# Attention scores of two key heads in 64-row halves of the TensorE array

## The chip, the cores and the metric

The kernel runs on one core of a Trainium2 chip. A core has TensorE (PE: matmuls, with its weight loads shown apart as PEld), VectorE (DVE), ScalarE (ACT), GpSimd (POOL) and SyncE (SP, which here issues the DMAs). TensorE writes into PSUM, eight banks of 128 rows by 512 f32 values; the others work from SBUF, and VectorE and ScalarE also read PSUM. The metric is the device time of one execution in microseconds.

## The reference

One layer of a decoder that runs windowed attention beside a state-space branch, then a gated feed-forward part with a short convolution, for a prompt of 2048 tokens and eight samples of four tokens. The attention of the prompt, which is what the change touches, is this (cut):

```python
qb = q.reshape(b, nb, BLOCK, N_KV_HEADS, GQA_GROUP, HEAD_DIM)   # 16 blocks of 128, 2 key heads, 4 query heads each, 64
kband = jnp.concatenate([kb[:, :-1], kb[:, 1:]], axis=2)        # the block before and this one: 256 keys
s = jnp.einsum('bnqhgd,bnkhd->bnhgqk', qb, kband) * scale
s = s - slopes * dist                                           # ALiBi
s = jnp.where(valid, s, MASK_VALUE)
p = _sink_softmax(s, sinks)
o = jnp.einsum('bnhgqk,bnkhd->bnqhgd', p.astype(v.dtype), vband)
```

`_sink_softmax` subtracts the maximum over the keys and the head's sink, takes the exponential, and divides by the sum with the sink's exponential added.

## The kernel before

The kernel works through stages. First it projects the inputs of the state-space branch for all tokens. Then, between about 150 and 530 us, it interleaves four kinds of work: the projections of queries, keys and values in tiles of 256 tokens, the state-space branch in 16 pairs of groups, the attention in 16 blocks of 128 queries, and, towards the end, the activations, the gate (`glu`) and the sample attention. Behind it come the output projection and the feed-forward part, which take the rest of the time and which the change does not touch.

**The order.** The interleaving is written out by hand. Each kind of work is a Python generator that is cut into steps by `yield`, and the string `ORDER` names one step after another: `q` the next step of the projections, `s5` the next step of pair 5 of the state-space branch, `a4` the next step of attention block 4, `g` a step of the gate, `x` of the sample attention, `e` of the activations, `Y` the loads for those. TensorE's instructions run in just this order (`manual_schedule` for that engine). The instructions of the other engines are ordered by the compiler's planner, by their place in the program and by what is ready; on each engine they then run in order. The numbers that the generators yield are not read when the order is written out.

**An attention block** (`attention_block`, L523) has five steps:

1. scores of key head 0 for its four query heads, their eviction, and the softmax of head 0;
2. the same for key head 1;
3. transposes of head 0's probabilities (`tp_b`, L556), eight of them in two banks, and copies to SBUF (`pT`);
4. the same for head 1;
5. the product with the values (`o`, L567), its copy and its DMA out.

**Scores.** A query tile holds, for each of four positions j, 128 rows: the 64 values of query head j of key head 0, and below them the 64 values of query head j of key head 1. To pick one key head out of it, the keys are padded: `kpad[i][:, kv, :]` has 128 rows of which the 64 of the other key head are zero. So a matmul takes all 128 rows with 256 keys as the moving side. Queries and keys are each split into a high and a low part (two fp32r tiles, index i), and `mm3` (L87) issues three matmuls into the same columns of a PSUM bank: high x high, high x low, low x high. A bank `sc` holds two query heads of 256 keys; there are two such banks. VectorE evicts each half bank with one operation (L545) that adds the bias, takes the maximum with the sink, and writes scores `s` and maximum `m`.

**Softmax** (`softmax`, L506) of one key head: VectorE negates the maximum (`ngm`), ScalarE takes four exponentials with their sums (L513), VectorE forms the sink's share and the reciprocal (`es`, `den`), and GpSimd multiplies the four heads (L520). Only then can the transposes of step 3 or 4 start. The `s` tiles lie in four buffers, so block b uses those of block b-2 again.

**Keys.** `kpads` (L840 on) are two pairs of key tiles of 384 keys each, used in turn by tiles of 256 tokens. GpSimd fills the rows of the other head with zeros once, and in the first pair also the 128 keys ahead of the prompt. The keys of each tile are then written by ScalarE and VectorE into the 64 rows of their head (L912 on), and GpSimd copies the last 128 keys of the tile before.

**The sample attention** (`sample_attention`) computes its scores in tiles of 64 rows by 32 columns of the array (L604), with the keyword `tile_position`, in f32.

## Time and profile before

| | |
|---|---|
| time, median of 3 runs | 2193.05 us (2192.98 to 2195.53) |
| the profiled execution's own time | 2194.39 us |
| its span, first to last instruction | 2192.2 us |
| mean granted TensorE clock | 0.973 |
| busy: PE / DVE / ACT / POOL | 2054.4 / 1307.6 / 1055.8 / 1208.9 us |

In the profile a row of the timeline gives start, length, engine, line, operation, output<-inputs, the form (rows*columns of the array for TensorE, then the output), and in brackets the idle time before it with what ended it. A TensorE instruction's length includes the way through the array, so that consecutive ones overlap; the distance of their starts is what one costs, and the chain of waits shows just that distance. The page's busy time of TensorE is a union of such lengths.

### The profile page before, as it was taken

The numbers are of one execution on the slowest core, as the hardware profiler recorded it, in microseconds if no ns is written. First come the engines' busy times: TensorE is split into PE (matmuls) and PEld (weight loads), VectorE is DVE, ScalarE is ACT, GpSimd is POOL, SyncE is SP. The second block draws the span as 40 slices with busy tenths as digits, with TensorE's granted clock in tenths as the row PEclk, the third lists the DMA queues.
The fourth block names the chain that finished last, engine by engine and source line by source line (L and its number), as shares of the span: only waits on it lengthen the run. The fifth ranks groups of instructions, "written<-read, shape, count | busy, mean of one in ns | idle before, by whom it ended". The sixth has DMA issues, their size and how long they took to land.

```text
span 2192.2 us, 41498 instructions
## 1 busy us (share of the span) xinstructions
PE 2054.4 (94%) x14685; PEld 1923.5 (88%) x14685; DVE 1307.6 (60%) x3298; ACT 1055.8 (48%) x2467; POOL 1208.9 (55%) x1196
## 2 busy tenths in 40 slices
PE   8969999968999979999999998999999999999997
PEld 8967878857998979999999786779999999888997
DVE  8859998458565576766766265227766766601231
ACT  6525465665454456666666332225655655612011
POOL 4857776334356776666665553446666666823121
PEclk9989999989999989999999999999999999999999
DMA  8865434686488733333334795834333333584643
GB/s 232 240 169 158 116 106 138 125 230 189 146 248 258 262 109 109 113 95 109 114 95 128 263 284 170 303 117 157 110 93 108 111 93 108 177 205 125 199 132 95
DMA packets 294352, 347.59 MB, mean 159 GB/s; under 512 B 42344, under 2 KB 250864, under 8 KB 294128
## 3 DMA queue, kind: packets, MB, share of 16 engines
q1 hardware_dynamic: 294144, 344.94, 52.3%
q8 instruction: 116, 1.90, 0.4%
q14 instruction: 92, 0.75, 0.1%
HBM read 232.70 MB, written 107.80 MB: 155 GB/s over the span
## 4 chain that ended last, share of the span: by engine, by line
PE 75%; DVE 8%; DMA 6%; issue 4%; ACT 3%; POOL 3%; SPq 2%; DVEq 0%; ACTq 0%; POOLq 0%
PE ux L1362 21%; PE u L1362 16%; PE dn L90 6%; PE dn L89 6%; PE dn L91 6%; PE wo L90 2%; PE wo L91 2%; PE wo L89 2%; PE qkv L89 2%; PE qkv L91 1%; PE qkv L90 1%; DVE xo L1444 1%; SPq L802 1%; PE u L91 1%; DMA mt<-mscr 1%
## 5 line engine op out<-in xcount | busy, mean ns | idle before, releaser
L84 POOL TENSOR_TENSOR wdl<-wdr,wdh 128x1024 fp32r<-128x1024 f32 x65 | 159.3, 2455 | 287.3 <-ACT wdh L83 272.0
L89 PE MATMUL dn<-ah,wdh 128*128 128x512 f32 (+3 forms) x552 | 205.6, 372 | 8.9 <-DMA ah<-actscr 3.6
L91 PE MATMUL dn<-ah,wdl 128*128 128x512 f32 (+3 forms) x552 | 205.1, 371 | 3.3 <-POOL wdl L84 3.3
L90 PE MATMUL dn<-al,wdh 128*128 128x512 f32 (+3 forms) x552 | 204.9, 371 | 0.5 <-DMA al<-actscr 0.5
L1327 ACT ACTIVATE cc<-u,cw 128x260 f32<-128x260 f32 (+1 forms) x252 | 141.5, 563 | 93.8 <-DVE u L1405 64.1
L1519 DVE TENSOR_TENSOR xo<-xo,dn 128x512 f32<-128x512 f32 (+3 forms) x40 | 21.9, 584 | 265.4 <-PE dn L91 265.1
L83 ACT CAST wdh<-wdr 128x1024 fp32r<-128x1024 f32 x65 | 68.0, 1050 | 230.4 <-PE dn L90 188.4
L84 POOL TENSOR_TENSOR wls<-s,whs 128x1024 fp32r<-128x1024 f32 x42 | 100.9, 2402 | 133.2 <-ACT whs L83 133.2
L1328 DVE SCALAR_TENSOR_TENSOR cc<-u,cw,cc 128x260 f32<-128x260 f32 (+1 forms) x252 | 121.0, 481 | 64.2 <-ACT cc L1327 62.7
L89 PE MATMUL wo<-mh,wo 128*128 128x260 f32 x512 | 149.0, 291 | 2.5 <-ACT mh L83 2.5
L90 PE MATMUL wo<-ml,wo 128*128 128x260 f32 x512 | 146.7, 287 | 1.5 <-POOL ml L84 1.3
L91 PE MATMUL wo<-mh,wo 128*128 128x260 f32 x512 | 146.4, 286 | 0.0
L1405 DVE TENSOR_TENSOR u<-u,cb 128x262 f32<-128x262 f32 x84 | 36.5, 435 | 158.5 <-PE u L1362 158.5
L89 PEld LDWEIGHTS dn<-ah,wdh 128*128 128x128 f32 x552 | 105.1, 190 | 28.7 <-issue 4.0
L91 PEld LDWEIGHTS dn<-ah,wdl 128*128 128x128 f32 x552 | 105.1, 190 | 20.8 <-POOL wdl L84 4.2
L89 PE MATMUL qkv<-hh_p,wqh 128*128 128x256 f32 (+1 forms) x384 | 113.5, 296 | 10.6 <-DVE vs L905 7.4
L84 POOL TENSOR_TENSOR wlt<-s,wht 128x512 fp32r<-128x512 f32 x42 | 54.1, 1288 | 122.6 <-ACT wht L83 64.0
L90 PEld LDWEIGHTS dn<-al,wdh 128*128 128x128 f32 x552 | 105.1, 190 | 17.6 <-DMA al<-actscr 1.0
L1329 DVE SCALAR_TENSOR_TENSOR cc<-u,cw,cc 128x260 f32<-128x260 f32 (+1 forms) x252 | 119.6, 475 | 0.8
L84 POOL TENSOR_TENSOR wlg<-wur,whg 128x1024 fp32r<-128x1024 f32 x42 | 101.1, 2407 | 27.8 <-ACT whg L83 27.8
L520 POOL TENSOR_SCALAR s_b<-s_b,den_b 128x256 f32<-128x256 f32 x128 | 75.4, 605 | 63.2 <-DVE den_b L518 38.4
L90 PE MATMUL qkv<-hl_p,wqh 128*128 128x256 f32 (+1 forms) x384 | 109.9, 286 | 0.0
(574 smaller groups left out, 8370.9 us busy)
## 6 DMA issues: line engine op xcount, KB each, us to landing
actscr<-cc SPq DMA_DIRECT2D x168, 260.0 KB, 4.9
wur<-in_w_up SPq DMA_DIRECT2D x84, 512.0 KB, 4.1
wdr<-in_w_down SPq DMA_DIRECT2D x77, 512.0 KB, 4.9
x<-in_xT SPq DMA_DIRECT2D x56, 256.0 KB, 4.2
hs<-h2scr SPq DMA_DIRECT2D x44, 262.0 KB, 4.6
ah<-actscr SPq DMA_DIRECT2D x42, 256.0 KB, 3.9
al<-actscr SPq DMA_DIRECT2D x42, 256.0 KB, 4.2
mt<-mscr SPq DMA_DIRECT2D x16, 520.0 KB, 5.5
```

Of the source, the lines that this page charges most:

```text
L83: i = nc.scalar.copy(hi, src) if hi_eng is nc.scalar else hi_eng.tensor_copy(hi, src)
L84: return i.ins, lo_eng.tensor_tensor(lo, src, hi.bitcast(F32), ALU.subtract).ins
L89: nc.tensor.matmul(ps, w[0], x[0], start=first, stop=False)
L90: nc.tensor.matmul(ps, w[0], x[1], start=False, stop=False)
L91: nc.tensor.matmul(ps, w[1], x[0], start=False, stop=last)
L520: nc.gpsimd.tensor_scalar(s[:, h], s[:, h], den[:, h : h + 1], 1.0, ALU.mult, ALU.mult)
L802: nc.sync.dma_start(uscr[8 * m + g].rearrange("(s h) c -> h s c", h=16), uperm[m][16 * g : 16 * g + 16])
L1327: nc.scalar.activation(cp, pp[:, 2:], AF.Identity, bias=w[3], scale=w[2])
L1328: nc.vector.scalar_tensor_tensor(cp, pp[:, 1 : npr + 1], w[1], cp, ALU.mult, ALU.add)
L1329: nc.vector.scalar_tensor_tensor(cp, pp[:, 0:npr], w[0], cp, ALU.mult, ALU.add)
L1362: nc.tensor.matmul(pt[:, :W], x[p][:, k], y[q][:, k], start=start and k + i == 0, stop=k == 3 and i == 2, skip_group_check=True)
L1405: v.tensor_tensor(c21[s], c21[s], cb[s][:, 0], ALU.add)
```

## The change

Both key heads' scores are now computed in one step. A matmul takes 64 rows: those of its key head, from the query tile and from the key tile, at the matching half of the array's rows (`tile_position=(64 * kv, 0)`). For two query heads of each key head the matmuls of key head 0 and key head 1 alternate, each into a bank of its own. The first step of a block covers query positions 0 and 1 of both key heads, the second positions 2 and 3; the softmax of both key heads is called in the second step. The number of matmuls, their 256 moving columns, the evictions, the softmax and the later steps stay as they were, and so does `ORDER`. The maxima `m` get eight buffers instead of three. The zeros in the other head's rows are not written any more; those ahead of the prompt are.

```diff
-    ss, pts = [], {}
+    ss, ms, pts = [], [], {}
     for kv in range(2):
         nm = f"b{b}_{kv}"
         s = pool.tile([P, 4, 256], F32, tag="s", name=f"s_{nm}", bufs=4)
-        m = pool.tile([P, 4], F32, tag="m", name=f"m_{nm}", bufs=3)
+        ms.append(pool.tile([P, 4], F32, tag="m", name=f"m_{nm}", bufs=8))
         if b == 0:
             v.memset(s[:, :, 0:P], MASK)
-        for hh in range(2):
-            pt = ps.tile([P, 512], F32, tag="sc", name=f"sc_{nm}_{hh}")
-            for h2 in range(2):
-                j = 2 * hh + h2
-                q = [qhl[i][:, j, qb : qb + P] for i in range(2)]
-                k = [kpad[i][:, kv, kb : kb + 256] for i in range(2)]
-                mm3(nc, pt[:, 256 * h2 : 256 * h2 + 256], q, k, True, True)
+        ss.append(s)
+    for hh in range(2):
+        sc = [ps.tile([P, 512], F32, tag="sc", name=f"sc_b{b}_{kv}_{hh}") for kv in range(2)]
+        for h2 in range(2):
+            for i, (x, y) in enumerate(((0, 0), (0, 1), (1, 0))):
+                for kv in range(2):
+                    r = slice(64 * kv, 64 * kv + 64)
+                    nc.tensor.matmul(sc[kv][:, 256 * h2 : 256 * h2 + 256], qhl[x][r, 2 * hh + h2, qb : qb + P],
+                                     kpad[y][r, kv, kb : kb + 256], start=i == 0, stop=i == 2, tile_position=(64 * kv, 0))
+        for kv in range(2):
+            s, m, pt = ss[kv], ms[kv], sc[kv]
             for h2 in range(2):
                 j = 2 * hh + h2
                 lo = P if b == 0 else 0
...
-        softmax(c, pool, s, m, 4, c.sink[:, 4 * kv : 4 * kv + 4], nm)
-        ss.append(s)
+            if hh:
+                softmax(c, pool, s, m, 4, c.sink[:, 4 * kv : 4 * kv + 4], f"b{b}_{kv}")
         yield 1.4
...
-            for t in kp:
+            for t in kp if i == 0 else ():
                 f = t.bitcast(F32)
-                nc.gpsimd.memset(f[64:128, 0, :], 0.0)
-                nc.gpsimd.memset(f[0:64, 1, :], 0.0)
-                if i == 0:
-                    nc.gpsimd.memset(f[0:64, 0, 0:P], 0.0)
-                    nc.gpsimd.memset(f[64:128, 1, 0:P], 0.0)
+                nc.gpsimd.memset(f[0:64, 0, 0:P], 0.0)
+                nc.gpsimd.memset(f[64:128, 1, 0:P], 0.0)
```

## The prediction

> **What bounds the kernel now.** I read the page's head first, then a table of stretches of the span, then the chain of waits between 160 and 530 us (start, length, what), then the instructions that touch the score tile `sc_b`.

> ```profile
> span 2192.2 us, 41498 instructions
> ```

> The stretches (their length, then busy us of PE, PEld, DVE, ACT and POOL, granted clock, DMA share, GB/s):

> ```profile
> 177.00:227.00 50.00, 45.65 (x318) 35.55 (x314) 49.62 (x163) 28.99 (x95) 36.95 (x71) 1.00 0.43 122
> 227.00:408.00 181.00, 178.92 (x1300) 150.07 (x1301) 154.82 (x499) 97.05 (x307) 117.89 (x222) 1.00 0.41 117
> 408.00:530.00 122.00, 98.25 (x719) 82.92 (x717) 70.79 (x203) 83.78 (x203) 47.31 (x72) 0.92 0.80 198
> ```

> ```profile
> 176.68 0.13 PE sc_b L91
> 176.83 0.35 DVE s_b L545
> ...
> 226.93 0.38 DVE cl_s L413
> 227.35 0.61 PE pk_s L420 x4
> 227.96 0.32 PE qkv L89
> ...
> 409.91 7.07 DMA y<-yscr
> ```

> The reader sees three stages that hold attention. From 177 to 227 us the chain runs on VectorE, busy 49.62 of 50 us (**stage 1**). From 227 to 409 us it runs on TensorE, busy 178.92 of 181 us, with VectorE at 154.82 (**stage 2**). From 409 to 530 us it goes through DMAs, ScalarE and all engines in turn (**stage 3**). After that no instruction of attention is left. So TensorE time saved in stage 2 is worth its full length, as long as nothing else makes TensorE wait; in stage 1 it is worth nothing.

> **The change part by part.**

> *1. Scores in halves.* The instructions on `sc_b`:

> ```profile
> L91 PE MATMUL sc_b<-kp,q x128: 274/283/415, 167.4 to 487.4; 128*128 128x256 f32 x128
> ```

> Three lines of 128 make 384 matmuls, 12 in each of 32 steps (16 blocks, two each). Each takes 0.12 us of the chain, a step 12 x 0.12 = 1.43 us. The count stays; each now uses 64 rows, and neighbours use different rows. Do halves run side by side? The sample attention already places 64-row matmuls:

> ```profile
> 473.70 0.18 PEld L604 LDWEIGHTS ssc<-kc,qs 64*32 64x32 f32 x16 [0.20 <-issue]
> 473.70 0.72 PE L604 MATMUL ssc<-kc,qs 64*32 64x288 f32 x16
> ```

> ```profile
> 237.64 0.44 PE py_s L497 x2
> L604 PE MATMUL ssc<-kc,qs x16: 402/415/427, 473.7 to 474.0; 64*32 64x288 f32 x16
> ```

> An f32 matmul shows as two instructions; on the full array one of 264 columns takes 0.44/2 = 0.22 us, so 288 columns take 0.24. Sixteen take 0.72 us, of which 0.42 is one alone: their starts lie within 0.30 us. Were only the four column strips parallel, the last of four rounds would start 3 x 0.24 = 0.72 us after the first. It starts 0.30 after: two rounds, so both row halves worked at once. I take a pair as 0.12 us, six pairs as 0.72.

> Leaving and entering full-array work costs something. On the chain:

> ```profile
> 230.99 1.87 PE o L567 x8
> ...
> 233.77 1.02 PE tp_b L556 x8
> ...
> 242.26 0.87 PE tp_b L556 x8
> 246.94 1.72 PE o L567 x8
> ```

> `o` works in 64-column tiles: 1.87 us behind full-array work, 1.72 behind other tiled work, so 0.15 to enter. `tp_b` takes 1.02 behind tiled work and 0.87 otherwise: 0.15 to leave. With the wider loads of `qkv` leaving costs 0.32 - 0.12 = 0.20 (at 227.96, above). Score loads are as wide, so I take 0.20 each way. A step becomes 0.72 + 0.40 = 1.12 us, 0.31 less; where one neighbour in the written order is tiled already, 0.51 less. In stage 2 lie 16 steps, 8 of each kind: 8 x 0.31 + 8 x 0.51 = **-6.6 us**. Bounds: -11.4 (16 x 0.71) if changing is free, +4.8 (8 x 0.40 + 8 x 0.20) if halves take turns.

> *2. The softmax of head 0 starts one step later.* Today head 0's softmax starts behind a block's first score step, head 1's behind the second. Now each step holds both heads' queries of two groups, so both wait for the second. The transposes of head 0 (`tp_b`, step 3) stay at their place in TensorE's written order. Look at block 4, second step, today head 1 alone:

> ```profile
> 262.32 0.28 PE L91 MATMUL sc_b<-kp,q 128*128 128x256 f32 x1
> 267.04 1.04 PE L556 MATMUL tp_b<-ident,s_b 128*128 128x128 f32 x8
> 266.04 0.47 DVE L545 CUSTOM_DVE_ANT_0 s_b<-sc_b,bias,sink 128x256 f32<-128x256 f32 x1
> 268.25 0.51 ACT L513 ACTIVATE s_b<-s_b,ngm_b 128x256 f32<-128x256 f32 x1
> 272.07 1.87 POOL L520 TENSOR_SCALAR s_b<-s_b,den_b 128x256 f32<-128x256 f32 x4 [0.54 <-DVE ngm_b L510]
> ```

> Scores end at 262.60, head 1's probabilities at 273.94: a **latency** of 11.3 us, 3.4 of it VectorE's backlog. Head 0's transposes start at 267.04, a **gap** of 4.4 us behind the scores. In the changed kernel head 0 is where head 1 was, so TensorE would wait. Behind the waiting transposes stand, in written order, the next block's scores and a projection, whose evictions VectorE then lacks. The shortest latency is that of block 12's first step:

> ```profile
> 410.64 0.28 PE L91 MATMUL sc_b<-kp,q 128*128 128x256 f32 x1
> 415.02 1.84 POOL L520 TENSOR_SCALAR s_b<-s_b,den_b 128x256 f32<-128x256 f32 x4 [5.05 <-ACT osb L570]
> ```

> It is 416.86 - 410.92 = 5.9 us. Read so from the timeline for all 16 blocks (the first and the last gap shown below), the gaps are 5.7, 5.7, 2.7, 12.2, 4.4, 6.9, 9.8, 6.8, 7.6, 9.8, 6.1, 11.3, 2.9, 3.9, 3.6, 12.1 us and head 1's latencies 7.9, 12.9, 12.6, 14.4, 11.3, 8.6, 9.9, 9.2, 9.6, 9.1, 7.7, 6.6, 6.9, 8.5, 9.6, 11.2.

> ```profile
> 176.52 0.28 PE L91 MATMUL sc_b<-kp,q 128*128 128x256 f32 x1
> 182.51 0.27 PE L556 MATMUL tp_b<-ident,s_b 128*128 128x128 f32 x1
> ...
> 487.35 0.28 PE L91 MATMUL sc_b<-kp,q 128*128 128x256 f32 x1
> 499.70 0.38 PE L556 MATMUL tp_b<-ident,s_b 128*128 128x128 f32 x2
> ```

> Stage 2 is blocks 4 to 11. With their own latencies the waits add up to 14.7 us, with 6 us everywhere to 1.6. While TensorE waits the others catch up, so I take 8 us, between the best and the median of these eight (9.15): 3.6 + 1.1 + 1.2 + 0.4 + 1.9 = **+8.2 us**. Stage 2 together: +1.6.

> Stage 1 (blocks 0 to 3): at 8 us TensorE waits 2.3 + 2.3 + 5.3 = 9.9 us. VectorE has a backlog of some 3 to 6 us there and first works it off; then it runs dry. I charge about half, **+4** (bounds 0 and +10).

> Stage 3: block 13's wait vanishes in a wait of 13.1 us behind it; block 12's mostly in one of 2.4.

> ```profile
> PE glu L89 <- ACT ghi L83: 13.1, 1, 13.1
> 430.63 0.39 PE L89 MATMUL qkv<-hh_p,wqh 128*128 128x256 f32 x1 [2.38 <-DVE f L894]
> ```

> ```profile
> 470.50 0.28 PE L91 MATMUL sc_b<-kp,q 128*128 128x256 f32 x1
> 474.34 0.33 PE L556 MATMUL tp_b<-ident,s_b 128*128 128x128 f32 x1
> ```

> Block 14's scores end at 470.8, its transposes start at 474.34: a wait of 4.4 at 8 us, at a place where the chain runs through these very steps. I charge **+3** for the stage (0 to +7).

> *3. Both banks at once.* A step now needs both `sc` banks free at its first pair, and VectorE empties them only behind the last matmul. In the view of `sc_b` today's waits for it are small (us, times):

> ```profile
>   DVE m_b L545: 3.3, 4
> ```

> I add nothing (0 to +1). The larger `m` buffers and the earlier claim on `s` cost nothing: the buffers' former block has always passed its step 4.

> *4. Zero padding.* Eight fills of 0.41 us on GpSimd go:

> ```profile
> L845 POOL MEMSET kp<- x4: 412/412/413, 125.1 to 128.4; 64x384 f32 x4
> ```

> The chain is on SyncE's DMA issues there: 0.

> **Sum:** 4 + 1.6 + 3 = +8.6 us. The profiled execution took 2194.39 us, 2.2 outside its span; the sum stands on it as 2203.0. The median shown is 2193.05, so the time is 2201.7, say **2202**; this case's own range is 2197 to 2210.

> A place where a rule weighs against the change: behind the 10.8 us in which TensorE sat idle up to 160 us, `qkv` pieces took 0.21 us for some 3.7 us, then 0.12; behind the 2.38 us wait above they took 0.12 at once.

> ```profile
> PE pre_s L457 <- DMA u_s<-uscr: 10.8, 1, 10.8
> 162.94 0.21 PE qkv L90
> ```

> [...]

> **The rivals.**

> *A, faster.* The waits hardly appear, because head 0's two evictions go ahead of head 1's and the chain behind them is as quick as block 12's 5.9 us. It decides from a latency of about 6.5 us down. Then stage 2 gives -6.6 + 1.6 = -5, the others 0: 2188; 2183 if changing the mode is free. For it: ScalarE and GpSimd have room (97 and 118 of 181 us). Against it: only 2 of the 16 second steps show 6.9 us or less.

> *B, no change.* At 7 us stage 2 waits 3.8 (-2.8 net), stage 1 gives +2, stage 3 +1: 2193.

> *C, the halves take turns.* Weight loads of one array may follow one another: 16 loads 64 columns wide with short matmuls take (1.12 - 0.22)/15 = 0.06 us each,

> ```profile
> 487.92 1.12 PE L629 MATMUL o_s<-spT,vc 128*64 128x32 f32 x16
> ```

> so 128 columns some 0.12 as an estimate, and a pair 0.24 as now. The 16 loads of the sample attention lie in 0.18 us, but are 32 wide and too short to tell. Then stage 2 loses 4.8 instead of gaining 6.6: 2202 + 11.4 = 2213. [...]

> **Chances.** A move of 0.2% (4.4 us) is about what a measurement of this kernel can tell from none. Forecast 0.42 (slower), A 0.25 (faster), B 0.21 (same), C 0.12 (slower): faster 0.25, same 0.21, slower 0.54. The range 2186 to 2214 leaves out the fast half of A and the upper ends of C and of the forecast.

> **What would show it.** Pairs of `sc_b` matmuls starting a few ns apart, 0.12 us from pair to pair, show part 1 right; 0.12 between single ones shows C. The transposes' wait for GpSimd's normalisation, today

> ```profile
>   POOL s_b L520: 7.3, 9
> ```

> that is 7.3 us in nine places, should grow to some 25; if it stays under 10, A holds. Stage 2 should be 181 to 184 us, against 176 in A. I'd be wrong if the compiler's order on VectorE put head 0's steps far ahead, or if the waits fell only where VectorE had backlog.

## The result, and the profile after

The changed kernel takes **2227.5 us** in the median of four runs (2225.4 to 2230.5), against 2193.6 us for the kernel before (four runs, 2193.0 to 2195.5). The ratio is 1.015, with a 95% interval of 1.0135 to 1.0165. The sign was as predicted. The size, 33.9 us, is four times the predicted 8.6, and the time lies outside the range. The profiled execution of the changed kernel took 2230.5 us, with a span of 2228.7.

First the loss by place. I cut both traces at the same work: the first score step, block 3's product `o`, block 11's product, and the first matmul of the output projection. The views are the tables of stretches, before and then after. Columns: stretch, length, busy us of PE, PEld, DVE, ACT, POOL, granted clock, DMA share, GB/s.

```profile
167.00:246.80 79.80, 75.10 (x539) 60.75 (x539) 76.24 (x242) 46.79 (x149) 61.52 (x114) 1.00 0.48 137
246.80:410.80 164.00, 162.28 (x1188) 136.97 (x1184) 137.78 (x454) 87.44 (x278) 102.30 (x194) 1.00 0.41 118
410.80:547.40 136.60, 108.77 (x783) 92.71 (x782) 85.86 (x227) 86.47 (x210) 51.50 (x76) 0.91 0.79 201
```

```profile
167.00:258.20 91.20, 77.73 (x537) 58.94 (x538) 75.85 (x242) 47.34 (x149) 58.75 (x114) 0.93 0.43 119
258.20:431.40 173.20, 160.87 (x1188) 128.68 (x1184) 136.31 (x451) 86.44 (x278) 100.03 (x194) 0.97 0.40 112
431.40:579.90 148.50, 114.20 (x783) 93.86 (x782) 86.33 (x227) 87.07 (x211) 51.16 (x76) 0.85 0.72 184
```

| work | length | TensorE not busy (length less PE busy) |
|---|---|---|
| up to block 3's product (mostly stage 1) | 79.8 to 91.2: +11.4 | 4.7 to 13.5: +8.8 |
| up to block 11's product (stage 2) | 164.0 to 173.2: +9.2 | 1.7 to 12.3: +10.6 |
| up to the output projection (stage 3) | 136.6 to 148.5: +11.9 | 27.8 to 34.3: +6.5 |

The three together lose 32.5 us. VectorE's busy time is the same in all three within 1.5 us, so nothing became dearer there. TensorE was not busy for 25.9 us more, and busy for 6.6 us more although its score steps got shorter.

The waits of TensorE in the changed kernel, in the same three stretches (total us, times, longest):

```profile
PE tp_b L560 <- POOL s_b L520: 10.8, 4, 5.0
...
PE tp_b L560 <- POOL s_b L520: 6.8, 4, 5.3
PE pre_s L457 <- ACT wk_s L423: 3.0, 2, 1.8
...
PE tp_b L560 <- POOL s_b L520: 10.9, 4, 4.0
PE glu L89 <- ACT ghi L83: 10.2, 1, 10.2
```

Before the change TensorE's transposes waited for GpSimd's normalisation in one place:

```profile
PE tp_b L556 <- POOL s_b L520: 2.3, 1, 2.3
```

Now they wait in 12, for 28.5 us. The wait that was to show it, which counts the weight loads too, grew from 7.3 to 70.5 us, where some 25 had been named (the view of `tp_b` in the changed kernel: us, times):

```profile
  POOL s_b L520: 70.5, 55
```

**The score step itself** did what was expected. From the view of `sc_b` and from the timeline of a step at full clock:

```profile
L541 PE MATMUL sc_b<-kp,q x384: 271/278/581, 167.0 to 514.2; 64*128 64x256 f32 x192
```

```profile
463.97 0.98 PE L541 MATMUL sc_b<-kp,q 64*128 64x256 f32 x12
```

Twelve matmuls lie in 0.98 us, of which 0.28 is the last one's own length: six pairs at about 0.12 us, against twelve single ones at 0.12 before. In the records the two matmuls of a pair start mostly 2 to 5 ns apart, and 17 ns at most, but for two pairs that waited for a bank.

**Block 4**, the prediction's example, shows the loss (timeline of the changed kernel: start, length, engine, line, operation, in brackets the idle time before and its releaser):

```profile
271.78 0.97 PE L541 MATMUL sc_b<-kp,q 64*128 64x256 f32 x12
...
276.99 0.47 DVE L549 CUSTOM_DVE_ANT_0 s_b<-sc_b,bias,sink 128x256 f32<-128x256 f32 x1
...
278.52 0.51 ACT L513 ACTIVATE s_b<-s_b,ngm_b 128x256 f32<-128x256 f32 x1 [3.37 <-DVE ngm_b L510]
...
282.34 1.86 POOL L520 TENSOR_SCALAR s_b<-s_b,den_b 128x256 f32<-128x256 f32 x4 [0.74 <-DVE den_b L518]
...
282.87 2.71 PE L560 MATMUL tp_b<-ident,s_b 128*128 128x128 f32 x8 [5.31 <-POOL s_b L520]
...
285.51 1.22 PE L541 MATMUL sc_b<-kp,q 64*128 64x256 f32 x8
```

Head 0's second pair of evictions starts at 276.99, 4.2 us behind the scores, because VectorE works through other things first. From the end of the scores to head 0's last normalisation pass 284.20 - 272.75 = 11.5 us, which is about what head 1 took at that place before (11.3). The prediction had charged 8.

Three things are paid here. First, 5.31 us of idle time. Second, the transposes take 2.71 us instead of 1.04: the first four come 0.45 us apart, at GpSimd's pace of one query head per instruction (1.86/4), since each can start when its head is normalised. Third, TensorE comes back at a granted clock of 0.50. This is the table of stretches around that wait (the granted clock is the first number behind the bracket of POOL):

```profile
277.60:282.80 5.20, 0.00 (x0) 0.00 (x0) 4.52 (x17) 4.28 (x19) 4.30 (x9) 0.84 0.55 183
282.87:285.50 2.63, 2.62 (x8) 1.47 (x8) 0.25 (x2) 0.76 (x2) 2.63 (x6) 0.50 0.03 6
285.50:286.80 1.30, 1.30 (x13) 1.29 (x12) 0.00 (x0) 0.58 (x1) 1.21 (x3) 0.50 0.00 0
286.80:288.00 1.20, 1.20 (x8) 0.97 (x7) 0.80 (x3) 0.00 (x0) 0.00 (x0) 0.50 0.00 0
```

The clock drops within the wait (mean 0.84), at 281.17, and stays at 0.50 until 288.0. The 2.5 us of dense work from 285.5 to 288.0 would have taken about half of that at a clock of 1.00, as an estimate from the 0.50; the starts of the `qkv` matmuls, 0.21 us apart up to 288.0 and 0.12 us behind it, give a little less of a gain. So one late softmax cost about 5.3 + 1.7 + 1.2 = 8.2 us, and its price in the prediction was 3.6.

### The profile page after: what moved, and what is told of

It reads as the page before. It is cut to its first block, busy times and chain, and to the rows that moved or that the text cites. A ratio compares the mean times of both kernels' runs of the same rounds, so it can differ in the third digit from the quotient of the medians.

```text
span 2228.7 us, 41491 instructions
## 1 busy us (share of the span) xinstructions
PE 2061.2 (92%) x14685; PEld 1914.8 (86%) x14685; DVE 1309.7 (59%) x3298; ACT 1056.1 (47%) x2467; POOL 1201.4 (54%) x1188
## 4 chain that ended last, share of the span: by engine, by line
PE 59%; DVE 4%; DMA 3%; POOL 2%; ACT 1%; issue 1%; SPq 0%; DVEq 0%; POOLq 0%; ACTq 0%
PE ux L1363 20%; PE u L1363 16%; PE dn L90 6%; PE dn L89 6%; PE dn L91 6%; DVE xo L1445 1%; PE wo L90 1%; PE wo L91 1%; PE wo L89 1%; DMA wdr<-in_w_down 1%; POOL wd L84 1%; DVE ss_fo L134 0%; DMA al<-actscr 0%; DMA mt<-mscr 0%; POOL wdl L84 0%
## 5 line engine op out<-in xcount | busy, mean ns | idle before, releaser
L89 PE MATMUL dn<-ah,wdh 128*128 128x512 f32 (+3 forms) x552 | 204.9, 371 | 8.4 <-DMA ah<-actscr 3.9
L91 PE MATMUL dn<-ah,wdl 128*128 128x512 f32 (+3 forms) x552 | 204.4, 370 | 3.3 <-POOL wdl L84 3.3
L90 PE MATMUL dn<-al,wdh 128*128 128x512 f32 (+3 forms) x552 | 204.2, 370 | 0.5 <-DMA al<-actscr 0.5
L83 ACT CAST wdh<-wdr 128x1024 fp32r<-128x1024 f32 x65 | 68.1, 1050 | 230.6 <-PE dn L90 182.0
L89 PE MATMUL wo<-mh,wo 128*128 128x260 f32 x512 | 148.8, 291 | 1.0 <-ACT mh L83 1.0
L90 PE MATMUL wo<-ml,wo 128*128 128x260 f32 x512 | 146.5, 286 | 0.5 <-POOL ml L84 0.4
L91 PE MATMUL wo<-mh,wo 128*128 128x260 f32 x512 | 146.4, 286 | 0.0
L89 PEld LDWEIGHTS dn<-ah,wdh 128*128 128x128 f32 x552 | 104.7, 190 | 28.1 <-issue 4.3
L89 PE MATMUL qkv<-hh_p,wqh 128*128 128x256 f32 (+1 forms) x384 | 116.0, 302 | 8.1 <-DVE vs L906 7.3
L91 PEld LDWEIGHTS dn<-ah,wdl 128*128 128x128 f32 x552 | 104.7, 190 | 20.7 <-POOL wdl L84 4.2
L90 PEld LDWEIGHTS dn<-al,wdh 128*128 128x128 f32 x552 | 104.6, 189 | 17.4 <-DMA al<-actscr 1.0
L90 PE MATMUL qkv<-hl_p,wqh 128*128 128x256 f32 (+1 forms) x384 | 111.5, 290 | 0.0
L91 PE MATMUL qkv<-hh_p,wql 128*128 128x256 f32 (+1 forms) x384 | 111.3, 290 | 0.0
```

What stands on the lines that cost most here:

```text
L83: i = nc.scalar.copy(hi, src) if hi_eng is nc.scalar else hi_eng.tensor_copy(hi, src)
L89: nc.tensor.matmul(ps, w[0], x[0], start=first, stop=False)
L90: nc.tensor.matmul(ps, w[0], x[1], start=False, stop=False)
L91: nc.tensor.matmul(ps, w[1], x[0], start=False, stop=last)
```

## The experiments

Two theories stood at first. **W**: the change loses because head 0's probabilities become ready one step later, at transposes that stayed where they were. **D**: two softmaxes of a block called in one place crowd the in-order engines. Times are medians; each ratio is against the kernel before on the same chip (medians there 2194.9 to 2196.0 us). Diffs are against the changed kernel unless said otherwise.

### 64 rows without the new order

Before's two steps and softmax places, with 64-row matmuls one head after the other and without the padding:

```diff
-                for kv in range(2):
-                    r = slice(64 * kv, 64 * kv + 64)
...
-            if hh:
-                softmax(c, pool, s, m, 4, c.sink[:, 4 * kv : 4 * kv + 4], f"b{b}_{kv}")
+                r = slice(64 * kv, 64 * kv + 64)
+                for i, (x, y) in enumerate(((0, 0), (0, 1), (1, 0))):
+                    nc.tensor.matmul(pt[:, 256 * h2 : 256 * h2 + 256], q[x][r], k[y][r], start=i == 0, stop=i == 2, tile_position=(64 * kv, 0))
+        softmax(c, pool, s, m, 4, c.sink[:, 4 * kv : 4 * kv + 4], nm)
```

> The kernel before with its order and its softmax places; only the score matmuls take 64 rows, one head after another, and the zero padding is gone. Theory W (the loss is TensorE waiting at the transposes for head 0's later softmax, and the half clock behind such waits): no new wait, only entering and leaving the tiled mode, 0.2 us each way, about 5 us in the stage from 227 to 409 us: 2195 to 2202 us. Theory H (64-row matmuls or the missing padding themselves cost the time): 2215 us or more.

Measured: 2202.5 us, ratio 1.0027 (1.0006 to 1.0048), 0.5 us above W's range and far from H's. Halves and missing zeros alone cost about a fifth of the loss (0.0027 of 0.0150), and here nothing of TensorE's time is saved.

### The new order without 64 rows

```diff
-                    nc.tensor.matmul(sc[kv][:, 256 * h2 : 256 * h2 + 256], qhl[x][r, 2 * hh + h2, qb : qb + P],
-                                     kpad[y][r, kv, kb : kb + 256], start=i == 0, stop=i == 2, tile_position=(64 * kv, 0))
+                    nc.tensor.matmul(sc[kv][:, 256 * h2 : 256 * h2 + 256], qhl[x][:, 2 * hh + h2, qb : qb + P],
+                                     kpad[y][:, kv, kb : kb + 256], start=i == 0, stop=i == 2)
```

with the padding of the keys put back.

> The changed kernel's order and late softmax, but full 128-row matmuls with the zero padding of before. Theory W: the waits stay, and each of 32 steps takes some 0.3 to 0.5 us longer than in the changed kernel: 2228 to 2240 us. Theory H: like before, 2190 to 2200 us.

Measured: 2229.2 us, ratio 1.0175 (1.0157 to 1.0192). The whole loss is there with full-row matmuls, and so is the wait (TensorE's waits between 167 and 545 us):

```profile
PE tp_b L559 <- POOL s_b L520: 25.8, 10, 6.4
```

So the loss belongs to the new distribution of scores and softmax over the steps, not to the halves. And what the halves save reaches the time only in small part: the two kernels' ratios differ by 0.0025, some 5.5 us (their intervals touch, so this is a rough figure), where 32 steps of 0.4 to 0.6 us less would be 13 to 19.

### All scores in the first step

```diff
-        sc = [ps.tile([P, 512], F32, tag="sc", name=f"sc_b{b}_{kv}_{hh}") for kv in range(2)]
+        sc = [ps.tile([P, 512], F32, tag="w" if hh else "sc", name=f"sc_b{b}_{kv}_{hh}") for kv in range(2)]
...
-        yield 1.4
+    yield 1.4
+    yield 0.0
```

> All scores of a block in its first step, row halves alternating, the second half of them in two banks of the pool that the other steps use; the second step is empty, and both softmaxes are called in the first step, 11 us or more ahead of the transposes. Theory W: no waits at the transposes, and a block's scores take some 1.8 us instead of 2.9: 2180 to 2192 us. Theory D (two softmaxes in one burst crowd VectorE, ScalarE and GpSimd, wherever they stand): 2205 us or more.

Measured: 2225.3 us, ratio 1.0151 (1.0127 to 1.0174). No transposes wait for GpSimd here any more, yet nearly all of the loss is there, with other waits:

```profile
PE glu L89 <- ACT ghi L83: 22.0, 2, 16.9
...
PE o L572 <- ACT pT_b L564: 4.4, 1, 4.4
```

One of them in the timeline: eight exponentials of both heads stand on ScalarE from 390.33 on, the copy of the transposes behind them, and the product behind the copy.

```profile
390.33 0.51 ACT L513 ACTIVATE s_b<-s_b,ngm_b 128x256 f32<-128x256 f32 x1 [2.67 <-DVE ngm_b L510]
...
394.46 1.04 ACT L564 COPY pT_b<-tp_b 128x512 f32<-128x512 f32 x2
...
395.08 2.82 PE L572 MATMUL o<-pT_b,vtok 128*64 128x512 f32 x5 [4.45 <-ACT pT_b L564]
```

This was a miss for W alone: a head 0 that is early isn't enough when head 1 comes with it.

### All scores in the first step, head 1's softmax in the second

As the last one, but head 0 is evicted and softmaxed in step 1 and head 1 in step 2 (the banks that are shared with the transposes now hold head 0; block 12's second step goes ahead of block 13's first):

```diff
+    sc = [[ps.tile([P, 512], F32, tag="sc" if kv else "w", name=f"sc_b{b}_{kv}_{hh}") for kv in range(2)] for hh in range(2)]
...
+    for kv in range(2):
+        s, m = ss[kv], ms[kv]
+        for hh in range(2):
+            pt = sc[hh][kv]
...
+        softmax(c, pool, s, m, 4, c.sink[:, 4 * kv : 4 * kv + 4], f"b{b}_{kv}")
+        yield 1.4
```

> All scores of a block in step 1, in alternating halves into four banks (head 0's two among the banks that the transposes use, head 1's two where the scores were); head 0 is evicted and softmaxed in step 1, head 1 is evicted and softmaxed in step 2, as before the change on VectorE, ScalarE and GpSimd; b12's second step is put ahead of b13's first. Theory W (the loss is head 0's softmax coming a step late) and theory D (two softmaxes emitted in one burst crowd the in-order engines) both foresee no loss of that kind here, since head 0 is as early as before and the bursts are as before: the step itself saves about 1 us a block, so 2183 to 2196 us. Theory H (what costs is the alternation itself, or two more banks held through a step): 2200 to 2225 us.

Measured: 2209.0 us, ratio 1.0058 (1.0035 to 1.0081). Against the last experiment 16 us come back by the medians, 20 by the ratios. The main difference is that head 1's evictions and softmax are called a step later, which is what D asks for; the banks and the place of one step changed with it and were not tried alone. But 13 us of loss are left, more than either theory foresaw. TensorE's longest waits inside attention are now for VectorE's evictions to free the banks, and for copies of the transposes:

```profile
PE o L572 <- ACT pT_b L564: 4.2, 4, 2.4
...
PE sc_b L541 <- DVE m_b L551: 2.9, 1, 2.9
```

That fits theory H of the expectation, but its parts (alternation, four banks) were not taken apart.

### The softmax call alone

The kernel before with one edit: head 0's softmax is called at the end of step 2.

```diff
-        softmax(c, pool, s, m, 4, c.sink[:, 4 * kv : 4 * kv + 4], nm)
         ss.append(s)
+        ms.append(m)
+        if kv:
+            for i in range(2):
+                softmax(c, pool, ss[i], ms[i], 4, c.sink[:, 4 * i : 4 * i + 4], f"b{b}_{i}")
```

> The kernel before with one edit: head 0's softmax is called at the end of step 2, right ahead of head 1's, instead of at the end of step 1. Padded full-row matmuls, one head after the other, order of steps, evictions: as before the change. Theory W/D (a late softmax and two in one burst carry all of the loss): 2222 to 2235 us, like the changed kernel. Theory S (the spread of each head's four evictions over two steps carries a good part): 2195 to 2212 us.

Measured: 2202.6 us, ratio 1.0030 (1.0013 to 1.0047), the number of theory S. The trace gives its reason. Head 0's maxima are complete after step 1 here, and the planner, which orders VectorE, ScalarE and GpSimd by what is ready, runs most of these softmaxes early although they are called late. In block 4 the first exponential starts 5 us ahead of step 2, which begins at 270.9:

```profile
265.86 0.51 ACT L513 ACTIVATE s_b<-s_b,ngm_b 128x256 f32<-128x256 f32 x1 [1.93 <-DVE ngm_b L510]
```

From block 4 to block 11 TensorE's steps start 9.2 to 10.2 us later than before the change, with no growth: stage 2 loses nothing. The 10 us are lost in blocks 1 and 2, where the transposes wait 2.9 and 3.9 us. There the planner did not run head 0's softmax early: in blocks 1 to 3 it ends 8.0 to 10.5 us behind step 2, where before the change it ended 1.1 to 4.8 us behind it. (They show in the trace; the median loses 6.5.) So in stage 2 it isn't the place of the call that costs. It costs when the **data** comes late: when head 0's maxima need the second score step, no planner can run it earlier.

### The order moved apart

Each block's second score step earlier and its third to fifth later, with at least 9 us between the second score step and head 0's transposes (one of the seven lines of `ORDER`):

```diff
-a4 s8 a4 a6 s7 a5 s9 q a6 s9 s8 s10 s9 q a5 a5 a6 q a7 s10 s9 s10 q s11 a6 a7 a6 s11 q s11 a7 q s10 s12 a7 a7
+a5 s8 a4 s8 a6 a4 s7 s9 q a5 a6 s9 s8 s10 s9 q a5 a5 q a6 a7 s10 s9 s10 q a7 s11 a6 s11 q a6 s11 q a7 s10
```

> The changed kernel with another written order: second score steps earlier, steps 3 to 5 later, so that at least 9 us of other TensorE work lie between a block's second step and its transposes. Theory W: the waits shrink to a few us, and the 0.3 to 0.5 us a step that the halves save come through: 2186 to 2200 us. Theory D: 2210 us or more.

Measured: 2223.6 us, ratio 1.0144 (1.0124 to 1.0164), outside W's range and inside D's. The transposes' wait is gone from the top of the list, and others stand there (TensorE's waits):

```profile
PE glu L89 <- ACT ghi L83: 21.3, 1, 21.3
PE pk_s L420 <- DVE cl_s L413: 9.2, 3, 5.4
PE qkv L89 <- DVE f L895: 7.0, 2, 4.1
```

I then called head 1's softmax one step later in this order:

```diff
-            if hh:
+            if hh and not kv:
...
+        if not kv:
+            softmax(c, pool, ss[1], ms[1], 4, c.sink[:, 4:8], f"b{b}_1")
```

> The kernel with the moved steps (second score steps earlier, third to fifth later), and head 1's softmax called behind head 0's transposes, one step after head 0's. Theory D (what was left with the moved steps is the two softmaxes in one burst): the loss falls to 2195 to 2212 us. Theory M (what was left is the moved order itself, or the evictions of both heads in one burst): 2215 us or more.

Measured: 2241.7 us, ratio 1.0214 (1.0186 to 1.0241). Worse, and no test of D after all: now head 1 is the late one.

```profile
PE tp_b L560 <- POOL s_b L520: 15.2, 6, 8.3
```

What is left in the moved order isn't settled. The evictions and softmaxes of both heads in one place are one candidate, the move of the steps another.

### The change in some blocks only

This is the test by dose. The prediction had listed, block by block, the distance from the second score step to head 0's transposes. Here the changed code runs in chosen blocks, before's code with padded keys in the others:

```diff
+HALVES = (3, 6, 9, 11, 15)
...
+    if b in HALVES:
...
+    else:
```

The five blocks with the widest distance:

> The change in five blocks alone, those with the widest distance from the second score step to head 0's transposes in the trace of before (blocks 3, 6, 9, 11, 15: 12.2, 9.8, 9.8, 11.3, 12.1 us); the other eleven blocks as before the change, with the padded keys. Theory W (a late head 0 costs only where this distance is shorter than the softmax takes): no wait in 9 and 11, at most 2 us each in 3, 6 and 15, some 0.8 us saved per block: 2189 to 2200 us. Theory G (every changed block costs about the same, 34/16 = 2.1 us): 2204 us or more.

Measured: 2199.5 us, ratio 1.0015 (1.0002 to 1.0028).

The five with the shortest:

> The change in the five blocks with the shortest distance (blocks 2, 4, 12, 13, 14: 2.7, 4.4, 2.9, 3.9, 3.6 us), the others as before the change. Theory W: in each a wait of 4 to 6 us ahead of head 0's transposes, those of 12 and 13 partly swallowed by waits behind them, and half the granted clock for some microseconds after each: 2208 to 2222 us. Theory G: 2204 us, as with the five widest.

Measured: 2212.3 us, ratio 1.0080 (1.0052 to 1.0108).

Blocks 6, 9 and 11 alone:

> The change in blocks 6, 9 and 11 alone, which lie where TensorE sets the pace and have 9.8, 9.8 and 11.3 us of distance. Theory W: no wait, six score steps at 0.3 to 0.5 us less each: 2.6 us less than before, 2190 to 2195 us. Theory G: 2199 us or more.

Measured: 2195.4 us, ratio 1.0000 (0.9986 to 1.0015).

The first two came within W's ranges, the third 0.4 us above it; G's 2204, 2204 and 2199 fit none of them. The same edit in the same number of blocks costs 17.4 us at short distances and 4.5 at wide ones, and theory G's even price would give the same for both. (The sets lie in different stages too: of the tight blocks only 4 is in stage 2, of the wide ones 6, 9 and 11. So the waits count more than the two totals.) TensorE's wait for the normalised heads over all of attention, first with the tight blocks, then with the three:

```profile
PE tp_b L586 <- POOL s_b L521: 21.6, 6, 6.8
```

```profile
PE tp_b L586 <- POOL s_b L521: 2.6, 2, 2.3
```

The second is as before the change (2.3 in one place), and the kernel with the five widest has the same line, so its 4.5 us are not waits for the softmax; where they come from was not found. In the tight kernel the waits ahead of head 0's transposes are 6.8, 5.4, 2.5, 2.8 and 2.6 us in blocks 2, 4, 12, 13 and 14; W had expected 4 to 6 in each, so its total fits better than its single waits. Block 4 again waits 5.4 us, and the padded full-row scores behind it run at a granted clock of 0.50:

```profile
277.21 2.70 PE L586 MATMUL tp_b<-ident,s_b 128*128 128x128 f32 x8 [5.40 <-POOL s_b L521]
...
281.20 0.42 PE L91 MATMUL sc_b<-kp,q 128*128 128x256 f32 x1
281.41 0.42 PE L92 MATMUL sc_b<-kp,q 128*128 128x256 f32 x1
```

Their starts are 0.21 us apart instead of 0.12. From the end of block 4's second score step to the end of block 5's first, TensorE's order falls back by 12.7 - 4.4 = 8.3 us, the price of one late softmax once more.

The three blocks gain nothing, although 2.6 us were to be had. Block 6 does gain 0.9 us. In blocks 9 and 11 the second step needs both banks at its first pair, and one of them isn't empty:

```profile
361.59 0.38 PE L543 MATMUL sc_b<-kp,q 64*128 64x256 f32 x1 [0.34 <-DVE m_b L551]
362.40 0.97 PE L543 MATMUL sc_b<-kp,q 64*128 64x256 f32 x11 [0.43 <-DVE m_b L551]
```

The first matmul starts at 361.59, its partner 0.81 us later. That is about what the step saves.

## Why the prediction was right in sign and wrong in size

- **What bounds the kernel**, right. Stage 2 runs on TensorE, and waits put there stay: the three blocks with distance and the five tight ones show that the loss follows the waits. But the proviso "as long as nothing else makes TensorE wait" was priced at nothing and did not hold (below).
- **Part 1, halves in pairs**, right: pairs at 0.117 us, and rival C (halves take turns) fell. At full clock a step with the changes of mode around it saves 0.4 to 0.6 us, a little more than the 0.31 and 0.51 that were priced: from the start of the instruction ahead of the step to the start of the one behind it, 1.55 us became 1.10 in block 1's first step and 1.74 became 1.11 in block 4's.
- **Part 2, right in mechanism, wrong in size.** Head 0's transposes do wait for its softmax. The 8 us of latency were a fair middle: read as in the prediction, head 0's latencies in the changed kernel are 7.5, 12.1, 9.0, 11.9, 11.5, 9.0, 7.3, 8.8, 7.9, 7.4, 7.3, 6.3, 7.1, 8.0, 9.2 and 9.4 us, the median 8.4, in stage 2 7.6. The reason given for them, "while TensorE waits the others catch up", failed where it mattered most: block 4 shows 11.5, about what head 1 had there, since the 4.2 us of VectorE's backlog pass before TensorE begins to wait and can't be worked off in it. Still, stage 2's waits add up to 6.8 us, where 8.2 were charged: 5.3 in block 4, 1.4 in block 5. The step that failed is that **a wait was charged with its idle time alone**. Left out were transposes at GpSimd's pace (1.7 us in block 4) and work at half clock behind them (an estimated 1.2 us), so that block 4 cost about 8 us where 3.6 were charged. Block 5 pays both without any wait above 0.54 us. Its transposes take 3.19 us instead of 1.04, and behind them the granted clock is 0.50 for 3.4 us, from 305.07 to 308.48, which costs 1.7 by the same estimate. This is the table of the two stretches:

```profile
301.69:304.88 3.19, 1.75 (x11) 1.18 (x11) 3.19 (x11) 1.24 (x4) 3.19 (x6) 1.00 0.63 149
304.88:308.48 3.60, 3.60 (x20) 3.60 (x19) 2.74 (x9) 0.73 (x2) 3.60 (x10) 0.53 0.90 278
```

Stage 2's +9.2 is nearly all made in blocks 4 and 5: TensorE's order is 11.4 us late ahead of block 4, 20.5 behind block 5's head 0, and 20.6 at block 11's product. From block 6 on the shorter score steps should have won some of it back. They won next to nothing: TensorE's other waits grew there by 3.8 us (1.6 before, 5.4 after), a term that the prediction put at nothing. These are the main ones, first before the change, then after it:

```profile
PE tp_b L556 <- DVE wk_s L426: 0.9, 1, 0.9
PE pre_s L457 <- ACT wk_s L423: 0.7, 1, 0.7
```

```profile
PE pre_s L457 <- ACT wk_s L423: 3.0, 2, 1.8
PE tp_b L560 <- ACT vtok L883: 1.3, 1, 1.3
PE sc_b L541 <- DVE m_b L549: 0.7, 2, 0.4
```

- **Stage 1**: in sum the waits were right, 9.9 us expected and 10.8 measured, but partly by luck: 2.3, 2.3, 5.3 and 0 were expected for blocks 0 to 3, and 0.9, 5.0, 4.9 and 0 came. "I charge about half, +4" was wrong. The loss is 11.4 us. VectorE was busy as long as before (75.9 and 76.2 us), but in 91.2 instead of 79.8 us: its backlog covered nothing.
- **Stage 3**: +3 predicted, +11.9 measured. I let blocks 12 and 13 vanish in waits behind them, but the transposes there still waited 10.9 us in four places (block 14 among them), the long wait for the gate shrank by 2.9 us only (13.1 to 10.2), and the granted clock of the stage fell from 0.91 to 0.85.
- **Part 3, banks**: nothing in the sum, and small it was (0.7 us in two places). Where the latency is covered it decides, as the last experiment shows.
- **Part 4, padding**: 0, as far as the first experiment can tell.
- **The clock** is not in the sum and belonged there. The row that the prediction set beside it, `qkv` pieces at 0.21 us for some 3.7 us behind the wait of 10.8 us, pointed the right way: the granted clock was 0.50 there up to 166.0 us, and it was 0.50 behind block 4's wait of 5.31 us and behind a wait of 2.51 us at block 12 too (last section).
- **Rivals A and B** would have needed latencies of 6.5 and 7 us; only block 11, with 6.3, is below 7.
- **A reading** in the prediction belongs to another step: 6.9 us, given as block 12's latency, is that of block 13's first step, and block 12's is 7.4. So one second step, not two, shows 6.9 or less. The sum doesn't use it.

The cause of the sign and of most of the size is shown: the new distribution of the scores loses as much with full-row matmuls (1.0175) as with halves (1.0150), and the same edit costs 17.4 us in the five blocks with the shortest distance against 4.5 in the five with the widest. The late softmax is the shown part of it. The six blocks between were not tried alone, and the kernels with all scores in the first step and with the moved steps lose as much almost without that wait. Why the orders with moved steps do no better, and what the 13 us of the split version are, stays open. No version tried beats the kernel before; the one with three blocks equals it.

## What to carry to other kernels

Before pairing two independent pieces of TensorE work to save array time, look at what each is waited for by: pairing makes the first as late as the second, and the distance to its reader, place by place, has to exceed the latency that the trace shows at that place, backlog of the other engines included. Price a new wait of TensorE as its idle time, plus a reader that restarts at its producer's pace, plus the stretch at half clock behind it: some 8 us here for 5.3 us of idle time. And a change that pays in some places and loses in others can be tried in those places alone, which is also the quickest way to learn whether one has the cause.

## What the runs showed of the hardware that was not expected

Two waits of nearly the same length, 2.51 and 2.38 us, were followed by different clocks. In the changed kernel a wait of 2.51 us at block 12 ended with transposes at GpSimd's pace, and the clock fell behind it. This is the table of stretches over the wait, the transposes and the projection (the granted clock is the first number behind the bracket of POOL):

```profile
444.50:447.00 2.50, 0.01 (x1) 0.01 (x1) 0.34 (x2) 2.50 (x12) 0.54 (x2) 1.00 1.16 133
447.00:449.30 2.30, 1.93 (x9) 1.36 (x9) 0.54 (x2) 1.64 (x8) 1.89 (x5) 0.81 1.15 143
449.30:451.00 1.70, 1.70 (x10) 1.70 (x9) 0.00 (x0) 1.43 (x3) 1.24 (x3) 0.50 0.84 162
```

```profile
445.02:448.42 3.40, 1.06 (x4) 0.49 (x5) 0.79 (x4) 3.20 (x16) 1.84 (x4) 1.00 1.16 134
448.44:451.83 3.39, 3.39 (x17) 3.39 (x18) 0.07 (x1) 2.67 (x4) 1.84 (x4) 0.50 0.83 153
```

```profile
428.84:432.24 3.40, 1.61 (x13) 1.61 (x14) 0.76 (x2) 3.39 (x5) 0.06 (x1) 1.00 0.34 115
432.26:435.66 3.40, 3.40 (x31) 3.40 (x30) 0.42 (x1) 3.40 (x7) 1.44 (x2) 1.00 0.74 258
```

```profile
557.38:560.77 3.39, 1.05 (x9) 0.84 (x8) 0.43 (x1) 2.43 (x7) 2.14 (x3) 1.00 0.63 211
560.79:564.19 3.40, 2.23 (x5) 1.34 (x5) 1.18 (x3) 1.51 (x4) 2.19 (x4) 0.50 0.00 0
```

In the first stretch TensorE was busy for 1.06 us, and the clock behind it was 0.50. In the second, around the wait of 2.38 us, it was busy for 1.61 us, and the clock stayed at 1.00. In the third it was busy for 1.05 us, and the clock behind it was 0.50. Over all such stretches at a clock of 1.00 between 160 and 2000 us in the traces of the kernel before and the changed kernel, all 27 with less than 1.5 us of busy TensorE were followed by 0.50, 3 of the 14 with 1.5 to 2.05 us, and none of the 973 with more. These are counts of two traces; why the clock fell behind 3 of those 14 and not behind the others is not shown. So the prediction's reading at its wait of 2.38 us, `qkv` pieces at 0.12 us at once, can't be carried over to other waits of that length: behind the wait of 2.51 us they took 0.21 us until 451.84.
